# Retention q, k and gate columns as six transposed pairs of seven half-size products, values as row projections

## The chip, the cores and the metric

The kernel runs on one core of a Trainium2 chip. TensorE (PE in the profile) multiplies, VectorE (DVE) and ScalarE (ACT) work on its results, GpSimd (POOL) helps with elementwise work and issues some DMAs, SyncE (SP) issues most of them. The metric is the device time of one execution in microseconds (us).

## The reference, cut to what matters

One decoder layer over 1024 rows of width 1024. A combined projection of the modulated input feeds eight forgetting-attention heads ("fox", 64 wide) and four retention heads (128 wide). Retention is computed in chunks of 128 rows:

```
h  = modulate(x)                                  # 1024 x 1024
q, k, v, f, rq, rk, rv, rg = split(h @ w_in)      # widths 3 x 512, 8, 4 x 512
rq, rk = rotate(rq), rotate(rk)                   # cos and sin of the position
per retention head and chunk:
    out   = (rq rk^T * inner) rv + (rq * xi) state
    state = g_chunk * state + (rk * zeta)^T rv
ret = group_norm(out) * swish(rg)
fox = softmax(q k^T / 8 + decay(f), causal) v
x   = layer_norm(alpha*x + gate * (concat(fox, ret) @ w_out)), then the MLP in the same manner
```

Everything is float32. A product of two float32 matrices is made of three matmuls of rounded parts, hi*hi + hi*lo + lo*hi.

## The kernel before, in words

The modulated input stands in SBUF transposed, as eight tiles `hhi` (the rounded part) and eight `hlo` (the rest) of 128 features x 1024 rows. A row projection takes 128 columns of these as the stationary operand and a 512 wide weight tile as the moving one: 8 feature blocks x 3 matmuls = 24 matmuls give 128 rows x 512 columns in one PSUM bank (`three`).

**First phase.** For each feature block j, `h_load` brings two 512 KB tiles `ada1`, which make the modulation, the weights `wrr` (256 KB) and the input `xt` (512 KB); ACT and DVE make `hhi` and `hlo`, and PE multiplies seven of the eight row chunks with `w0`, 21 matmuls for each j, into seven PSUM banks. In the kernel before `w0` holds the q, k, v and gate columns of retention head 0. All loads of this phase stand in one order on SP. Behind the last `xt` come the weights of head 1 (`wrr_0` to `wrr_3`, 512 KB each), of which the first is cast on ACT ahead of `hhi` of j = 7.

**Retention rows.** For each head and chunk one row projection of 512 columns (q, k, v, gate of that head): a copy to SBUF, the rotation on DVE (and POOL), then `ret_a` (q and k turned by PE, k scaled on ACT as `kz`), `ret_b` (scores and state product), `ret_c` (output and statistics), `ret_swish`. Once eight chunks of a head are done, `ret_norm` makes scale and offset from the statistics (17 small DVE operations for a head), `ret_gate` applies them on ACT, two chunks in a step, and multiplies by the gate on POOL, and `ret_out` turns the result and stores it to `mixR`. A table of ticks sets which of these steps is written between which halves of the row projections.

**Values of fox.** Behind that 16 row projections of 256 or 264 columns (`v_proj`) make the fox values (kept in SBUF as `V2`) and the forget gate. Meanwhile 32 pieces of the modulation for later stages (`mod_piece`, one DVE operation of 128x1024 each) are worked off.

**Fox.** Then come the projections of fox head 0 (`fox_proj`, 24 matmuls of 512 columns for each half t of the rows, in four parts): t = 0 and one part of t = 1 ahead of the loop, the other three parts in the loop's steps i = 0 to 2, then score blocks, softmax, turns and products.

**What sets the order.** Operations issued through `in_turn`, `turn` and `vec` keep the order in which they are written, on PE and on DVE. In the first phase the loads on SP and the work of ACT are pinned in the same way (`queued`). What ACT, POOL and SP issue besides in this block is put in order by a scheduler at build time (the block is opened with `schedule_with_timeline_sim`); each engine then works through its own queue strictly in order.

## Time and profile before

| | before |
|---|---|
| three runs | 1214.98, 1216.07 and 1216.07 us; median 1216.07 us |
| profiled execution, first to last instruction (no other time of it is listed) | 1214.8 us |
| PE busy | 1198.3 us, 99% |
| DVE busy | 910.9 us, 75% |
| ACT busy | 653.9 us, 54% |
| POOL busy | 229.0 us, 19% |
| first phase | 0 to about 50.7 us |
| retention rows | 50.7 to 222.4 us |
| fox values | 222.4 to 272.3 us |
| fox head 0, its projections | from 272.3 us |

An engine's share is an average over all stages. A wait in a row stands behind the instruction that waited, with the engine that ended the wait. A matmul's row shows its time in the pipe, several overlap; how fast PE works is read from a run of them (12 in 2.75 us).

### The profile page before, as it was taken

Reading aid. Unit: us, or ns where it says so; the run is one execution under the profiler, and the core shown is the slowest. Engines: PE = TensorE matmul, PEld = TensorE weight load, DVE = VectorE, ACT = ScalarE, POOL = GpSimd, SP = SyncE. Lnnn points to the kernel's source line nnn. Section 1 sums busy time; section 2 is a strip of 40 time slices with the busy share of each in tenths; the row PEclk is TensorE's granted clock in tenths of the full one; section 3 lists DMA queues with packets and bytes.
Section 4 is the critical chain, followed back from the end, with each engine's and each line's share of the span. In section 5 each row is a group of like instructions: output and inputs, shape, how many; then the busy total and the mean of one; then the engine's idle time right before and its main releaser. Section 6 shows DMA issues by size and latency. Waiting matters only on the chain.

```text
span 1214.8 us, 17196 instructions
## 1 busy us (share of the span) xinstructions
PE 1198.3 (99%) x6005; PEld 1002.4 (83%) x6005; DVE 910.9 (75%) x1757; ACT 653.9 (54%) x1201; POOL 229.0 (19%) x274
## 2 busy tenths in 40 slices
...
GB/s 358 227 87 122 139 148 143 202 32 175 164 222 164 203 171 335 96 77 115 87 178 204 193 223 185 171 184 175 152 139 128 148 249 297 321 243 178 248 181 69
DMA packets 94279, 216.57 MB, mean 178 GB/s; under 512 B 10784, under 2 KB 17136, under 8 KB 94192
## 3 DMA queue, kind: packets, MB, share of 16 engines
...
## 4 chain that ended last, share of the span: by engine, by line
PE 87%; DMA 5%; DVE 4%; ACT 1%; issue 1%; SPq 0%; POOL 0%; DVEq 0%; ACTq 0%; POOLq 0%
PE rp L152 11%; PE dX L1489 7%; PE uX L1264 7%; PE uX L1263 7%; PE uX L1265 7%; PE dZ L1489 5%; PE uY L1263 5%; PE uY L1265 5%; PE uY L1264 5%; PE vp L152 4%; PE pv L851 3%; DMA ada<-in_ada_dram 3%; PE pt L835 2%; PE op L189 2%; PE op L191 2%; PE op L190 2%
## 5 line engine op out<-in xcount | busy, mean ns | idle before, releaser
L152 PE MATMUL rp<-wr,hhi 128*128 128x512 f32 x400 | 127.9, 401 | 0.0
L1475 DVE TENSOR_TENSOR dl<-dr,dh 128x1024 fp32r<-128x1024 f32 x66 | 80.3, 1237 | 36.3 <-ACT dh L1463 35.1
L813 POOL TENSOR_TENSOR S<-S,dn 128x128 f32<-128x128 f32 (+3 forms) x64 | 73.5, 1154 | 151.7 <-DVE dn L812 130.1
L1463 ACT CAST dh<-dr 128x1024 fp32r<-128x1024 f32 x58 | 59.6, 1051 | 65.7 <-DMA dr<-td 35.5
...
L152 PEld LDWEIGHTS rp<-wr,hhi 128*128 128x128 f32 x400 | 71.6, 189 | 12.7
L152 PE MATMUL rp<-wr,hlo 128*128 128x512 f32 x200 | 78.6, 393 | 0.0
L1489 PE MATMUL dX<-dh 128*128 128x512 f32 x176 | 68.5, 389 | 0.8 <-DVE ds L1641 0.8
L1489 PE MATMUL dX<-dl,dh 128*128 128x512 f32 x176 | 68.5, 389 | 0.0
L1489 PE MATMUL dX<-dh,dl 128*128 128x512 f32 x176 | 68.5, 389 | 0.0
L1278 ACT COPY u<-uX 128x512 f32<-128x512 f32 x44 | 25.8, 586 | 70.3 <-PE uX L1265 70.3
L152 DVE CUSTOM_DVE_ANT_0 ada<-ada,csb,bcol 128x1024 f32<-128x1024 f32 x46 | 60.1, 1309 | 3.0 <-DMA ada<-in_ada_dram 3.0
L842 DVE TENSOR_TENSOR pt<-pt,pt 128x512 fp32r<-128x512 f32 (+2 forms) x96 | 50.7, 549 | 10.2 <-ACT pt L841 9.1
L809 ACT ACTIVATE S<-S,mn 128x128 f32<-128x128 f32 (+3 forms) x64 | 49.9, 779 | 11.1 <-DVE mn L802 10.5
L765 PE MATMUL qk<-hhi,wqh 128*128 128x512 f32 x128 | 54.8, 428 | 0.4 <-DVE pt L828 0.4
L767 PE MATMUL qk<-hhi,wql 128*128 128x512 f32 x128 | 51.9, 405 | 0.0
L1489 PE MATMUL dZ<-dh 128*128 128x512 f32 x132 | 51.6, 391 | 0.0
L1489 PE MATMUL dZ<-dl,dh 128*128 128x512 f32 x132 | 51.4, 389 | 0.0
L1489 PE MATMUL dZ<-dh,dl 128*128 128x512 f32 x132 | 51.4, 389 | 0.0
L841 ACT CAST pt<-pt 128x512 fp32r<-128x512 f32 (+2 forms) x96 | 44.1, 478 | 13.4 <-PE pt L835 12.1
L189 PE MATMUL op<-wo,mxs 128*128 128x512 f32 x128 | 51.1, 399 | 0.0
L802 DVE CUSTOM_DVE_ANT_0 S<-ps,nb 128x128 f32<-128x128 f32 (+3 forms) x64 | 47.4, 741 | 4.2 <-PE ps L800 3.5
...
## 6 DMA issues: line engine op xcount, KB each, us to landing
...
```

Of the source, the lines that this page charges most:

```text
L152: order[key] = fn(*args, **kw)
L189: mm(pt, ahi, whi, start=start, stop=False)
L765: nc.tensor.matmul(pt, whi[:, j, :], hhi[j][:, sl], start=(j == 0), stop=False)
L767: nc.tensor.matmul(pt, wlo[:, j, :], hhi[j][:, sl], start=False, stop=(j == ND - 1))
L813: nc.gpsimd.tensor_tensor(out=Ssb[:, :span], in0=Ssb[:, :span], in1=den.to_broadcast([P, span]), op=ALU.mult,)
L842: nc.vector.tensor_tensor(out=dl, in0=src, in1=f(dh), op=ALU.subtract)
L1263: nc.tensor.matmul(pt, whi, bh, start=start, stop=False, skip_group_check=True)
L1264: nc.tensor.matmul(pt, whi, bl, start=False, stop=False, skip_group_check=True)
L1265: nc.tensor.matmul(pt, wlo, bh, start=False, stop=stop, skip_group_check=True)
L1463: nc.scalar.copy(hi, raw)
L1475: nc.vector.tensor_tensor(out=lo, in0=raw, in1=f(hi), op=ALU.subtract)
L1489: nc.tensor.matmul(pt, w_[:, 0, q], m_[:, 1, :], start=start and n_ == 0, stop=stop and n_ == 2, skip_group_check=True)
```

## The change

It does the following.

- `w0` of the first phase now holds the 512 value columns of fox; the chunks are taken in the order 4, 5, 6, 7, 0, 1, 2, and chunk 3 follows. `fv_out` splits them and stores them to DRAM (`V2d`); eight DMAs of POOL bring them back as `V2` at the end of the block.
- `w1` holds the retention values of all four heads: eight row projections of 24 matmuls, stored to `rv_d` and read back for each head by `r_begin`.
- The forget gate becomes two products of 16 matmuls (`forget_proj`, 16 or 8 rows x 512) and eight small turns.
- The 12 blocks of 128 columns of q, k and gate form six pairs. Each pair is computed transposed (features on the partitions, 1024 rows along the free axis) as seven products of half size, after Strassen and Winograd: the sums of weight halves are made on POOL (`rw_s`, `rw_d`, `rw_z`), the sums of the input's halves once by POOL and DVE (`t_sums`, `t_first`), and each product is 4 feature blocks x 3 = 12 matmuls. `r_evac` adds the products together.
- `t_first` overwrites the second halves of `hhi` and `hlo` of j = 0 to 3; `h12_save` stores them to DRAM before (8 x 256 KB, issued on SP), `h12_load` brings them back at the end with eight DMAs of POOL.
- The rotation works on transposed tiles: `spin` swaps the halves with two ACT copies and multiplies on POOL, `spin_end` does the rest on DVE. Of q and k only k is turned, and not in the last chunk. The gate (`swish`, `swish_end`, `r_gate`) is multiplied on DVE from PSUM.
- `r_norm` issues the eight ACT operations of a head (scale and offset, 128x128) in one step.
- Both halves t of the projections of fox head 0 stand at the end of the block, and the loop has none of head 0 left for i = 0 to 2.

The core of the diff (the removed functions are in the listing above):

```diff
+RPAIRS = [
+    [("q", 0), ("k", 0)], [("q", 1), ("k", 1)], [("g", 0), ("g", 1)],
+    [("q", 2), ("k", 2)], [("q", 3), ("k", 3)], [("g", 2), ("g", 3)],
+]
...
+    def h12_save(j):
+        for u, t in enumerate((hhi[j], hlo[j])):
+            nc.sync.dma_start(h12d[u, j], f(t[:, 512:S]))
...
+    def r_prod(p, g, half, pt, start, stop):
+        whi, wlo = W["r", p, g]
+        for j in (2 * half, 2 * half + 1):
+            bh, bl = r_moving(g, 0, j), r_moving(g, 1, j)
+            a, b = start and j == 0, stop and j == 3
+            in_turn(pt, whi[:, j, :], bh, start=a, stop=False, skip_group_check=True)
+            in_turn(pt, whi[:, j, :], bl, start=False, stop=False, skip_group_check=True)
+            in_turn(pt, wlo[:, j, :], bh, start=False, stop=b, skip_group_check=True)
...
+    def r_norm(h, part):
...
+        for c in range(NT):
+            o = st["o"][:, c, :]
+            nc.scalar.activation(o, o, AF.Identity, scale=r[:, c:c + 1], bias=mr[:, c:c + 1])
...
+    for b, c in enumerate(CO):
+        fv_out(c, first[b])
+    for j in range(4):
+        h12_save(j)
...
+    START = {0: 18, 1: 34, 2: 60, 3: 75}
+    for h in range(RH):
+        p = (0, 1, 3, 4)[h]
+        wide = (2, 2, 2, 1)[h]
+        at(START[h] - 2, r_begin, h)
+        for c in range(NT):
+            t = START[h] + wide * c
+            at(t, r_scores, h, c)
+            at(t + wide, r_state, h, c)
+            at(t + (5 if wide == 2 else 2), r_rows, h, c)
+        t = START[h] + 7 * wide + (6 if wide == 2 else 3)
+        at(t, r_norm, h, 0)
+        at(t + 1, r_norm, h, 1)
+        for n in range(2):
+            at(max(t + 3 + n, 14 * (2 if h < 2 else 5) + 17 + h % 2), r_gate, h, n)
+
+    GROUPS = (1, 2, 6, 5, 7, 3, 4)
...
+    for p in range(NP):
+        st = {"X": bank(f"rX{p}"), "YZ": bank2(f"rY{p}")}
+        for gi, g in enumerate(GROUPS):
...
+            for half in range(2):
+                tick = 14 * p + 2 * gi + half
+                emit(tick)
+                r_prod(p, g, half, pt, g in (1, 2, 5), g in (2, 3, 4))
+            r_evac(p, g, st, tick)
...
+            if gi % 2 == 1 or gi == 6:
+                mod_piece("VM")
...
+    tick = 14 * NP
+    for t in range(2):
+        for part in range(4):
+            emit(tick)
+            tick += 1
+            if (t, part) == (0, 2):
+                mod_rows(1)
+            fox_proj(0, w, T[0], t, part, in_turn)
```

SP's queue at the end of the first phase, before: `wrr_7` is the weight of j = 7 (named `wrr_7` with a number of the tile), `wrr_0_345` the first load of `w1`.

```order
L152 DMA xt_294<-in_xT_dram 128x1024
L152 DMA ada_7_0_327<-in_ada_dram 128x1024
L152 DMA ada_7_1_328<-in_ada_dram 128x1024
L152 DMA wrr_7_331<-in_w_ret_dram 128x512
L152 DMA xt_333<-in_xT_dram 128x1024
L152 DMA wrr_0_345<-in_w_ret_dram 128x1024
```

The same place in the changed kernel; `hlo_264`, `hhi_261` and `hlo_303` are tiles of j = 2 and 3.

```order
L158 DMA xt_294<-in_xT_dram 128x1024
L158 DMA ada_7_0_327<-in_ada_dram 128x1024
L158 DMA ada_7_1_328<-in_ada_dram 128x1024
L441 DMA h12d<-hlo_264 128x512
L441 DMA h12d<-hhi_261 128x512
L158 DMA wrr_7_331<-in_w_fv_dram 128x512
L158 DMA xt_333<-in_xT_dram 128x1024
L441 DMA h12d<-hlo_303 128x512
L158 DMA wrr_0_345<-in_w_rv_dram 128x1024
```

Three of the eight stores are seen here; the other five stand between the loads of j = 4 to 6, so all eight are ahead of `wrr_0_345`.

ACT where head 0 is normalised, before: `rst` rows of head 0 are scaled by `L504`, those of head 1 are at chunks 4 to 6.

```order
L432 ACTIVATE kz_5_1226<-rst_2_591,rc 128x128
L428 COPY qkT_4_1146<-pq_4_1143 128x256
L504 ACTIVATE rst_0_496<-rst_0_496,mr_1100,gr_1050 128x128 x2
L504 ACTIVATE rst_1_497<-rst_1_497,mr_1100,gr_1050 128x128 x2
L473 ACTIVATE rst_2_591<-rst_2_591 128x128
L178 CAST wr_6_1110<-wrr_6_1108 128x512
L178 CAST wr_7_1113<-wrr_6_1108 128x512
L466 COPY rst_0_589<-po_1_1129 128x128
L395 COPY rst_3_592<-rp_7_1116 128x512
L466 COPY rst_1_590<-po_2_1170 128x128
L432 ACTIVATE kz_6_1280<-rst_3_592,rc 128x128
```

ACT at that place in the changed kernel: `ro_1194` is the output of head 0, `kz_3_1670` the scaled k of chunk 3 of head 1, `rwD3h` the rounded weight sum of pair 3, `th` a tanh of the gate, `ru` the finished columns of a pair, `rX` a PSUM bank of a product.

```order
L634 ACTIVATE kz_2_1605<-pa_2_1600,rc 128x128
L660 COPY ro_1489<-po_0_1623 128x128
L554 CAST rwZ_1696<-rwa_1397 128x512
L686 ACTIVATE ro_1194<-ro_1194,mr_1639,gr_1608 128x128 x8
L520 CAST rwD3h<-rwb_1480 128x1024
L604 ACTIVATE th_1656<-ru_0_1475 128x512
L895 COPY ru_1_1476<-rX_1402 128x512
L634 ACTIVATE kz_3_1670<-pa_3_1665,rc 128x128
L660 COPY ro_1489<-po_1_1678 128x128
```

The eight operations of a head stand in one row of the queue, ahead of a cast, a tanh, a copy and `kz_3`; before they were in groups of two and four between the others.

DVE where head 2 is normalised, before: `gt`, `gr` and `wg` are the root's small tiles, `mr` the offset, the chunk operations are those of head 3.

```order
L152 TENSOR_SCALAR wg_1999<-wg_1999 128x8
L152 TENSOR_TENSOR gr_1996<-gr_1996,wg_1999 128x8
L152 TENSOR_SCALAR gr_1996<-gr_1996,rc 128x8
L152 SCALAR_TENSOR_TENSOR mr_2056<-mv_1200,gr_1996 128x8
L152 SCALAR_TENSOR_TENSOR rst_0_1824<-rst_0_1824 128x128
L152 TENSOR_TENSOR rst_1_1825<-rst_1_1825,trig 128x256
L152 TENSOR_TENSOR rst_1_1825<-rst_1_1825,rt_3_2071 128x2x64 x2
L152 ISA ada_2_3_2008,gcol<-ada_2_3_2008,csb,bcol 128x1024
L152 ISA gcol 128x1
L152 BN_STATS bs_1_2119<-po_1_2116 128x6
L152 BN_AGGR mv_1828<-bs_1_2119 128x2
```

DVE at that place in the changed kernel: `ru_0_2316` is a gate block of pair 5, `ISA ada` a `mod_piece`, `po_5` an output and `R_6` a state of head 3.

```order
L158 TENSOR_SCALAR wg_2508<-wg_2508 128x8
L158 TENSOR_TENSOR gr_2505<-gr_2505,wg_2508 128x8
L158 TENSOR_SCALAR gr_2505<-gr_2505,rc 128x8
L158 SCALAR_TENSOR_TENSOR mr_2548<-mv_2020,gr_2505 128x8
L158 TENSOR_TENSOR ru_0_2316<-rY_2238,r_5_2366 128x512
L158 ISA ada_3_6_2418,gcol<-ada_3_6_2418,csb,bcol 128x1024
L158 ISA gcol 128x1
L158 BN_STATS bs_5_2578<-po_5_2575 128x6
L158 BN_AGGR mv_2302<-bs_5_2578 128x2
L158 SCALAR_TENSOR_TENSOR R_6_2584<-R_5_2529,rc,pb_6_2582 128x128
L158 TENSOR_TENSOR sT_7_2588<-pa_7_2586,dec_2299 128x128
```

The statistics, the state and the masked scores of head 3's chunks now stand behind the small operations, an addition of 512 columns and a `mod_piece`; before a chunk of head 3 had its own projection between them.

More of the change, by code (lines that the diff above doesn't have):

```diff
@@ L420, with fv_out @@
-    turned = {}
-    def ret_a(h, c, st):
-        row = st["st"][c // 2][:, c % 2, :]
-        pq = bank(f"pq{h}_{c}")
-        turn(pq[:, 0:128], row[:, 0:P], ident)
-        turn(pq[:, 128:256], row[:, P:2 * P], ident)
-        qkT = tmp([P, 256], F32, f"qkT{h}_{c}")
-        turned["last"] = nc.scalar.copy(qkT, pq[:, 0:256])
-        st["qkT", c] = qkT
+    def fv_out(c, pt):
+        vs = slot("S" if c % 2 else "R", [P, FH // 2, 2, P], F32R, f"vs{c}")
+        hv = pt.rearrange("p (g o d) -> p g o d", o=2, d=64)
+        for o in range(2):
+            a, b = (0, 64) if o == 0 else (64, 0)
+            hi = vs[:, :, o, a:a + 64]
+            nc.scalar.copy(hi, hv[:, :, o, :])
+            vec(nc.vector.tensor_tensor, out=vs[:, :, o, b:b + 64],
+                in0=hv[:, :, o, :], in1=f(hi), op=ALU.subtract)
+        nc.sync.dma_start(V2d.rearrange("h p c d -> p h c d")[:, :, c, :],
+                          f(vs.rearrange("p g o d -> p (g o) d")))
@@ new lines, in mod_rows, with mod_piece, w_gate @@
+    def mod_rows(m):
+        pt = bank(f"gT{m}")
+        turn(pt[:ND, :P], gcol[:, m, :], ident)
+        row = tmp([ND, P], F32, f"grow{m}")
+        nc.scalar.copy(row, pt[:ND, :P])
+        nc.sync.dma_start(gates[m:m + 1, :].rearrange("o (j p) -> (o j) p", p=P), row)
+    def mod_piece(tag="R"):
+        n = mst.get("n", 0)
+        m, j = divmod(n, ND)
+        if m < 4:
+            mod_part(m, j, mst["next"])
+            mod_load(n + 1, tag)
+            mst["n"] = n + 1
+    def w_gate():
+        w = sp.tile([P, ND, 2, FH], F32R, tag="dec", bufs=1, name="wg")
+        raw = wgr[:, 0:64].rearrange("p (j h) -> p j h", h=FH)
+        nc.scalar.copy(w[:, :, 0, :], raw)
+        vec(nc.vector.tensor_tensor, out=w[:, :, 1, :], in0=raw,
+            in1=f(w[:, :, 0, :]), op=ALU.subtract)
+        return w.rearrange("p j u h -> p j (u h)")
@@ new lines, with forget_proj @@
+    L = cp.tile([P, NT, FH], F32, tag="L", name="L")
+    cum_d = dp.tile([64, P], F32, tag="cum_d", name="cum_d")
+    def forget_proj(n, wg):
+        sl = slice(n * 512, n * 512 + 512)
+        pt = bank(f"pf{n}")
+        for j in range(ND):
+            in_turn(pt[:2 * FH], wg[:, j, :], hhi[j][:, sl], start=(j == 0), stop=False,
+                    skip_group_check=True)
+            in_turn(pt[:FH], wg[:, j, 0:FH], hlo[j][:, sl], start=False, stop=(j == ND - 1),
+                    skip_group_check=True)
+        t = tmp([2 * FH, 512], F32, f"fT{n}")
+        nc.scalar.copy(t, pt[:2 * FH])
+        return t
@@ new lines, in forget_rows, with forget_out @@
+    def forget_rows(n, t, pt):
+        for i in range(4):
+            c = 4 * n + i
+            turn(pt[:, c * 2 * FH:(c + 1) * 2 * FH], t[:, i * P:(i + 1) * P],
+                 ident[:2 * FH, :2 * FH])
+    def forget_out(pt):
+        src = pt[:, 0:2 * FH * NT].rearrange("p (c u h) -> p c u h", u=2, h=FH)
+        vec(nc.vector.tensor_tensor, out=L, in0=src[:, :, 0, :],
+            in1=bfb.unsqueeze(1).to_broadcast([P, NT, FH]), op=ALU.add)
+        vec(nc.vector.tensor_tensor, out=L, in0=src[:, :, 1, :], in1=L, op=ALU.add)
@@ L636, in fox_w @@
-    def fox_w(h):
-        raw = slot("R", [P, ND, P], F32, f"wqkr{h}")
-        nc.sync.dma_start(raw, w_qk[h])
-        whi = slot("X", [P, ND, P], F32R, f"wqh{h}")
-        wlo = slot("X", [P, ND, P], F32R, f"wql{h}")
-        nc.scalar.copy(whi, raw)
-        for q in range(2):
-            sl = slice(4 * q, 4 * q + 4)
-            nc.vector.tensor_tensor(
-                out=wlo[:, sl, :], in0=raw[:, sl, :], in1=f(whi[:, sl, :]), op=ALU.subtract
-            )
-        return whi, wlo
-    L = cp.tile([P, NT, FH], F32, tag="L", name="L")
@@ new lines, in r_gate @@
+    def r_gate(h, n):
+        st, sl = sts[h], slice(n * 512, n * 512 + 512)
+        pt = bank(f"py{h}_{n}")
+        for i in range(4):
+            turn(pt[:, i * P:(i + 1) * P], st["o"][:, 4 * n + i, :], ident)
+        g = st["g"][:, sl]
+        vec(nc.vector.tensor_tensor, out=g, in0=pt, in1=g, op=ALU.mult)
+        nc.sync.dma_start(mixR[h, :, sl], g)
+    RANK = (r_begin, r_rows, r_state, r_scores, spin_end, swish_end, r_norm, r_gate)
+    for b, c in enumerate(CO):
+        fv_out(c, first[b])
```

599 lines of the change are left out of this document (328 added, 271 removed).

## The prediction

> **What bounds the kernel now.** First the page: the span, the busy shares and their course.
>
> ```profile
> span 1214.8 us, 17196 instructions
> PE 1198.3 (99%) x6005; PEld 1002.4 (83%) x6005; DVE 910.9 (75%) x1757; ACT 653.9 (54%) x1201; POOL 229.0 (19%) x274
> ```
>
> PE is busy nearly throughout, so work taken from it shortens the kernel as long as nobody else is late instead. Whether PE really never waits in the stage that is changed, and how near the others are, is read from windows (span, then busy time and count of PE, weight loads, DVE, ACT, POOL, then granted clock, DMA share, GB/s).
>
> ```profile
> 40.00:45.00 5.00, 5.00 (x23) 3.86 (x21) 4.25 (x8) 2.41 (x5) 0.00 (x0) 1.00 1.03 403
> 45.00:50.00 5.00, 4.45 (x20) 3.64 (x20) 3.35 (x6) 4.77 (x8) 0.00 (x0) 1.00 0.53 190
> ...
> 50.00:100.00 50.00, 50.00 (x264) 42.62 (x263) 30.12 (x103) 20.00 (x57) 11.41 (x18) 1.00 0.25 76
> 100.00:150.00 50.00, 50.00 (x273) 42.89 (x272) 37.80 (x122) 23.21 (x67) 21.44 (x31) 1.00 0.41 127
> 150.00:200.00 50.00, 50.00 (x262) 42.22 (x261) 31.38 (x95) 20.85 (x57) 21.47 (x32) 1.00 0.46 144
> 200.00:250.00 50.00, 50.00 (x351) 46.60 (x350) 35.89 (x123) 22.05 (x75) 11.33 (x18) 1.00 0.54 172
> ```
>
> From 50 to 250 us PE has not one idle spot; DVE stands at 60 to 76%, ACT under half. Up to 45 us the bound is another: the DMA engines are full (share 1.03 at 403 GB/s). The chain of waits, in order of time, shows where the two bounds meet and what a matmul costs.
>
> ```profile
> 34.30 8.95 DMA wrr<-in_w_ret_dram
> ...
> 43.80 0.61 ACT wr L152
> 44.41 1.15 ACT hhi L152
> ...
> 45.61 1.20 PE fa L152 x4
> ...
> 56.35 2.75 PE rp L152 x12
> ...
> 239.27 14.48 PE vp L152 x120
> ```
>
> The last round of the first phase begins at 45.61, behind `hhi`, behind a cast, behind a load. A matmul of 512 columns takes 2.75/12 = 0.229 us, one of 256 or 264 columns 14.48/120 = 0.121 us.
>
> **PE's work.** Behind the first phase the kernel before has 25 row projections of 24 (600 matmuls of 512 columns), 16 x 24 = 384 narrow ones, and 48 of fox head 0. The changed one has the row projection of chunk 3 (24), eight of retention values (192), the forget gate (32), six pairs of seven products of 12 (504), and the same 48. The difference: 752 x 0.229 - 600 x 0.229 - 384 x 0.121 = -11.7 us. The turns:
>
> ```profile
> 68.75 0.38 PE L152 MATMUL pS<-qkT 128*128 128x128 f32 x2
> 68.97 0.39 PE L152 MATMUL pS<-rst,kz 128*128 128x128 f32 x2
> 69.19 0.38 PE L152 MATMUL pq<-ident,rst 128*128 128x128 f32 x2
> 69.33 0.71 PE L152 MATMUL rp<-wr,hhi 128*128 128x512 f32 x2
> ```
>
> By the starts, a product of 128 columns (two records) takes 0.22 us and two turns 0.14. 64 become 28, so -36 x 0.07 = -2.5 us, and eight small turns of the gate add about 0.5: **-13.7 us** in all, if nobody is late. This holds to a few tenths, as PE waits for nothing there now.
>
> **The first phase.** Eight stores of 256 KB (2.1 MB) now stand on SP ahead of `wrr_0`, the load that releases the cast ahead of the last `hhi`. DMA is full there, so they cost 2.1 MB / 0.404 MB per us = 5.2 us on the path that PE waits for. If they fit beside the loads they cost nothing, and if stores are slower than loads a little more: 0 to 6, I take **+5.2**, since the row shows no spare share. Moving `trig` and `dec` out helps nothing: they were issued behind `wrr_0`.
>
> **The stage of products.** From here the question is what stands between PE's own instructions. Durations:
>
> ```profile
> L152 DVE CUSTOM_DVE_ANT_0 ada<-ada,csb,bcol 128x1024 f32<-128x1024 f32 x32 | 42.2, 1320 | 0.7 <-DMA ada<-in_ada_dram 0.7
> L152 DVE BATCH_NORM_STATS2 bs<-po 128x6 f32<-128x128 f32 x32 | 9.4, 294 | 17.3 <-PE po L152 17.0
> L152 DVE TENSOR_TENSOR sT<-pS,dec 128x128 f32<-128x128 f32 x32 | 8.6, 269 | 3.4 <-PE pS L152 3.4
> L152 DVE SCALAR_TENSOR_TENSOR R<-R,rc,pS 128x128 f32<-128x128 f32 x24 | 8.1, 338 | 0.0
> L152 DVE BATCH_NORM_AGGREGATE mv<-bs 128x2 f32<-128x6 f32 x32 | 5.8, 182 | 1.0
> L152 DVE TENSOR_SCALAR wg<-wg 128x8 f32<-128x8 f32 x12 | 3.5, 295 | 0.3
> L152 DVE TENSOR_TENSOR wg<-gr 128x8 f32<-128x8 f32 x12 | 3.3, 276 | 0.2
> L152 DVE TENSOR_TENSOR wg<-wg,gt 128x8 f32<-128x8 f32 x12 | 3.0, 251 | 0.3
> L644 DVE TENSOR_TENSOR wql<-wqkr,wqh 128x512 fp32r<-128x512 f32 x4 | 2.6, 683 | 0.5 <-ACT wqh L641 0.5
> L152 DVE TENSOR_TENSOR gr<-gr,wg 128x8 f32<-128x8 f32 x12 | 2.6, 218 | 0.3
> ...
> L152 DVE TENSOR_SCALAR gr<-gr,rc 128x8 f32<-128x8 f32 x4 | 1.1, 270 | 0.1
> L152 DVE TENSOR_SCALAR gt<-gt,rc 128x8 f32<-128x8 f32 x4 | 0.9, 229 | 0.1
> L152 DVE TENSOR_SCALAR gt<-mv,rc 128x8 f32<-128x8 f32 x4 | 0.9, 225 | 0.0
> L152 DVE TENSOR_SCALAR gr<-gt 128x8 int32<-128x8 int32 x4 | 0.7, 172 | 0.1
> L152 DVE SCALAR_TENSOR_TENSOR mr<-mv,gr 128x8 f32<-128x8 f32 x4 | 0.7, 164 | 0.1
> ```
>
> The 17 small operations of one head's normalisation take 3 x (0.276 + 0.251 + 0.295 + 0.218) + 0.225 + 0.229 + 0.172 + 0.270 + 0.164 = 4.18 us. An operation of 512 columns takes 0.68, a `mod_piece` 1.32. On ACT and POOL:
>
> ```profile
> L395 ACT COPY rst<-rp 128x512 f32<-128x512 f32 x25 | 14.6, 585 | 26.3 <-PE rp L152 26.3
> L504 ACT ACTIVATE rst<-rst,mr,gr 128x128 f32<-128x128 f32 x32 | 13.3, 487 | 2.0 <-DVE mr L152 2.0
> L432 ACT ACTIVATE kz<-rst,rc 128x128 f32<-128x128 f32 x28 | 11.3, 405 | 31.1 <-DVE rst L152 17.5 <-PE pS L152 13.5
> ...
> L641 ACT CAST wqh<-wqkr 128x1024 fp32r<-128x1024 f32 x2 | 2.1, 1050 | 1.6 <-DMA wqkr<-in_w_qk_dram 1.6
> ...
> L179 POOL TENSOR_TENSOR wr<-wrr,wr 128x512 fp32r<-128x512 f32 x16 | 20.4, 1299 | 20.3 <-ACT wr L178 20.3
> ```
>
> Eight operations of `r_norm` are 8 x 0.487 = 3.9 us of ACT in one piece. At five places I add up what has to run between two instructions of PE, and what PE has to do meanwhile:
>
> - **Head 0 normalised, in pair 2.** From the end of the seventh product (g = 7): DVE does an addition 0.68, R 0.34, sT 0.27, the 17 small ones 4.18, bs and aggr 0.48, a swish 0.68, to `mr`: 6.6 us. Then ACT: eight operations 3.9, cast of `rwD3` 1.05, tanh 0.59, copy 0.59, `kz_3` 0.41: 6.5 us. PE waits for `kz_3` with `pb_3`; until then it has 24 matmuls (5.5 us) and some small ones (1.6 us), 7.1 us. Late by 13.1 - 7.1 = **6.0**.
> - **Head 1, start of pair 4.** From the end of the product g = 3: DVE 0.68 + 1.32 + 2 x 0.68 + 4.18 = 7.5, then four operations on ACT 1.9 until `py_0` is through. PE has 18 matmuls, 4.1 us. **5.4**.
> - **Head 2, among the chunks of head 3.** These follow each other at half the distance. From the end of g = 7 of pair 5 to `R_6` DVE has two whole chunks (bs, aggr, R, sT: 1.08 each) and most of a third (0.81), two additions and a swish (2.0), the small ones 4.18 and a `mod_piece` 1.32: 10.5. PE has 18 matmuls and 13 small ones, 6.9 us. **3.6**.
> - **Head 3, behind the last product.** From `po_6`: bs, aggr twice, two swishes, a `mod_piece`, the small ones, and 0.7 us for a tanh that stands behind the eight operations of head 2, 8.5 us; ACT 1.9. PE has 30 matmuls and the turns, 7.9 us. **2.5**.
> - **The first scores (pair 1).** `pa_0` waits for the last quarter of k: ACT 1.05 + 0.59 and two half swaps, POOL 2.6 (a tile of 1024 columns, taken as twice 1.3), 1.3 for the next sum and 1.3 for the product, DVE 0.68: 6.9 against 24 matmuls, 5.5. **1.4**.
>
> Together 18.9 us. Elsewhere DVE is the next bound. In a pair with six chunks it has four `mod_piece` (5.3), work of 14 times 512 columns (9.5), the chunks (6.5) and a normalisation (4.2), 25.5 us; PE has 84 matmuls and six chunks of 0.95, 24.9. It can be late by 1 or 2 us more between pairs 1 and 2, or the waits above may let it catch up. I take nothing for it. The bounds of these waits are 8 (if half of what is named is already done) and 25 (if the cross-engine hops and DVE's backlog come on top).
>
> **The start of fox.** Now 18 matmuls stand among the first score steps (4.1 us):
>
> ```profile
> 280.82 0.47 PE L796 MATMUL ps<-ks,qh 128*128 128x256 f32 x2
> ...
> 286.79 0.28 PE L835 MATMUL pt<-ident,S 128*128 128x128 f32 x1
> ```
>
> From scores to the first turn pass 6.0 us, filled with them. After the change only six of the next head are there. Between 0 and 4.1, I take half: **+2.0**. The reloads by POOL I cost at nothing: PE has eight parts (48 matmuls, 11 us) to cover them. If that is not enough, head 0's products wait for `V2`, some 2 us.
>
> **The sum.** -13.7 + 5.2 + 18.9 + 2.0 = +12.4, against the profiled span of 1214.8: 1227.2. The runs lie 0.2 to 1.3 us above that span, so **1228 us**.
>
> **Rivals.**
> - *The waits at the normalisations do not reach PE.* ACT is under half busy, and the same 17 and 8 operations of a head cost PE nothing in the rows above. If all four places (17.5 us) vanish, the time is 1228 - 17.5 = 1210.5; it is faster once they make less than 3 us. Against it: in the kernel before 24 matmuls stood between two chunks, now 12 or 6, and ACT's eight operations are in one piece. Chance 0.22.
> - *Half of it.* Waits of about 8 us and stores that cost half: 1228 - 11 - 2.5 = 1214.5 to 1218, within 0.2% of before. 0.10.
> - *PE's clock falls behind a long wait.* The granted clock is 1.00 in every row above, and before there is no long wait to see it fall. The two waits over 5 us would each be followed by some 3.4 us at half pace, if that is what happens: +3.4, 1231.5; with DVE's backlog 1235. 0.12.
>
> The Trainium skill, page "TensorE: Matmul & The Clock Gate", section "Part 1: The HAM clock gate (the "warmup" mystery)", states that an idle window of about 3.4 us puts the array on half its clock until it has been busy for as long; by it that last rival would be the forecast. No wait of before is long enough to show it.
>
> My forecast (1220 to 1232) has 0.56. A difference of 0.2% (2.4 us) is about what a measurement of this kernel can tell from no change. Faster: 0.22; within: 0.10; slower: 0.68. The range that leaves two in ten out reaches into the first rival and over the last: 1208 to 1236.
>
> **What would show it.** PE's idle time in front of `pb_3` of head 1, `py_0` of head 1, `po_6` of head 3 and `py_0` of head 3, released by ACT (or by DVE for `po_6`); the first phase ending some 5 us later than 50.7, with the stores between the loads; idle PE behind the first `ps`. The PE work is right if busy time falls by about 14 us. If PE is idle for less than 10 us in the stage of products, the hand sums of waits are wrong; if `fa` of the last round begins near 45.6, the stores cost nothing.

## The result and the profile after

The changed kernel takes 1267.17 us (median of four runs, 1266.41 to 1272.82), the kernel before 1216.07: a ratio of 1.0429, 95% interval 1.0407 to 1.0450. Slower was forecast, but by 12 us and not by 51; the range ended at 1236.

The page of the changed kernel, span, busy shares, and the slices of PE and of its granted clock:

```profile
span 1264.4 us, 16514 instructions
PE 1203.7 (95%) x5745; PEld 987.3 (78%) x5745; DVE 967.9 (77%) x1662; ACT 671.2 (53%) x1132; POOL 273.9 (22%) x246
...
PE   8999798698999999999999999999999999999997
...
PEclk9999799898999999999999999999999999999999
```

PE has less to multiply, yet its busy time rose from 1198.3 to 1203.7 us: a matmul at a lower clock is busy for longer (0.63 us in its row instead of 0.39). DVE's rose by 57 us. The two deepest holes in PE's slices (7 and 6 tenths, ahead of the last slice) lie between 120 and 260 us, and the windows show their size (columns as in the prediction):

```profile
50.00:100.00 50.00, 47.26 (x203) 35.15 (x204) 36.04 (x55) 26.51 (x53) 12.89 (x7) 0.97 0.60 188
100.00:150.00 50.00, 44.61 (x188) 36.05 (x187) 37.09 (x66) 14.85 (x22) 19.28 (x12) 0.93 0.53 182
150.00:200.00 50.00, 41.58 (x213) 34.57 (x214) 38.93 (x78) 19.18 (x40) 26.12 (x15) 0.93 0.37 122
200.00:250.00 50.00, 35.93 (x174) 29.56 (x173) 40.45 (x84) 23.44 (x49) 22.98 (x14) 0.86 0.35 113
```

Before, PE was busy for 50 of 50 us in each of these, at a clock of 1.00. Now it is idle up to 14 us of 50, and no other engine is busy for more than 41. That is the picture of chains between engines, not of one full engine. PE's timeline names the waits (start, duration, instruction, and in brackets the idle time ahead of it with the engine that ended it):

```profile
50.80 1.20 PE L158 MATMUL fa<-wr,hhi 128*128 128x512 f32 x4 [1.22 <-ACT hhi L158]
...
129.24 0.80 PE L158 MATMUL rY<-hhi,rwS0h 128*128 128x512 f32 x1 [4.03 <-DVE ru L158]
...
154.99 0.76 PE L158 MATMUL pa<-ru,ru 128*128 128x128 f32 x2 [6.35 <-DVE ru L158]
...
208.16 0.49 PE L158 MATMUL pb<-rv,kz 128*128 128x128 f32 x2 [3.81 <-ACT kz L634]
...
246.61 1.62 PE L158 MATMUL py<-ident,ro 128*128 128x128 f32 x4 [10.25 <-ACT ro L686]
...
289.67 0.49 PE L158 MATMUL pb<-rv,kz 128*128 128x128 f32 x2 [3.01 <-ACT kz L634]
...
310.79 0.49 PE L158 MATMUL po<-rv,sT 128*128 128x128 f32 x2 [1.98 <-DVE R L158]
...
331.89 0.66 PE L969 MATMUL ps<-ks,qh 128*128 128x384 f32 x1 [3.15 <-DVE mn L975]
```

**An account of the 49.6 us between the two profiled spans.** PE's work -13.7 (the prediction's figure; the last experiment below bears it out within 1.4 us); the last round of the first phase begins at 50.80 and not at 45.61, +5.2; idle time of PE between 50 and 330 us, summed over windows of 10 us, 39.9 against 0.6, +39.3; between 330 and 1100 us 4.2 against 2.0, +2.2. The clock: each such window's busy time times what its granted clock lacks of 1.00, summed, 14.0 against 0. Together 47.0; 2.6 us stay unassigned.

So three things are to be explained: why the waits hold twice what the hand sum gave, what the clock does, and whether the first phase's 5 us count.

### Where the longest wait comes from

The head's small operations run just ahead of the wait of 10.25 us. DVE's timeline of the changed kernel (start, duration):

```profile
234.89 1.60 DVE L158 TENSOR_TENSOR ru<-ru,sw 128x512 f32<-128x512 f32 x1
236.42 2.31 DVE L158 TENSOR_SCALAR gt<-mv,rc 128x8 f32<-128x8 f32 x1
238.76 1.18 DVE L158 TENSOR_SCALAR gt<-gt,rc 128x8 f32<-128x8 f32 x1
239.98 1.19 DVE L158 TENSOR_SCALAR gr<-gt 128x8 int32<-128x8 int32 x1
241.20 0.17 DVE L158 TENSOR_TENSOR wg<-gr 128x8 f32<-128x8 f32 x1
241.40 1.12 DVE L158 TENSOR_TENSOR wg<-wg,gt 128x8 f32<-128x8 f32 x1
242.55 1.19 DVE L158 TENSOR_SCALAR wg<-wg 128x8 f32<-128x8 f32 x1
243.77 0.17 DVE L158 TENSOR_TENSOR gr<-gr,wg 128x8 f32<-128x8 f32 x1
```

and POOL's timeline at the same time:

```profile
235.94 2.76 POOL L524 TENSOR_TENSOR rwD4l<-rwb,rwD4h 128x1024 fp32r<-128x1024 f32 x1
238.66 1.25 POOL L591 TENSOR_TENSOR sw<-sw,tab 128x512 f32<-128x512 f32 x1
239.88 1.25 POOL L535 TENSOR_TENSOR rws<-rwb 128x512 f32<-128x512 f32 x1
241.21 1.28 POOL L537 TENSOR_TENSOR rws<-rws,rwa 128x512 f32<-128x512 f32 x1
242.45 1.26 POOL L544 TENSOR_TENSOR rwb<-rwa,rwb 128x512 f32<-128x512 f32 x1
```

Five operations on eight columns (the two `gt`, `gr` and two `wg`), which take 0.17 to 0.23 us when POOL is idle, end when POOL's operation ends: 236.42 + 2.31 = 238.73 beside 235.94 + 2.76 = 238.70; 239.94 beside 239.91; 241.17 beside 241.13; and so on. Four of the five read a single tile. The `wg` at 241.20 began 0.01 us ahead of POOL's next operation and was not held. The row at 243.77, with POOL done, is back at 0.17. The 17 operations take 9.6 us and not the 4.2 of the prediction. That is one place; how much of the whole loss is this, the experiments tell.

### The profile page after: what moved, and what is told of

Same layout as the page of the kernel before. It is cut to its first block, busy times and chain, and to the rows that moved or that the text cites. A ratio compares the mean times of both kernels' runs of the same rounds, so it can differ in the third digit from the quotient of the medians.

```text
span 1264.4 us, 16514 instructions
## 1 busy us (share of the span) xinstructions
PE 1203.7 (95%) x5745; PEld 987.3 (78%) x5745; DVE 967.9 (77%) x1662; ACT 671.2 (53%) x1132; POOL 273.9 (22%) x246
## 4 chain that ended last, share of the span: by engine, by line
PE 63%; DVE 15%; DMA 13%; ACT 5%; issue 3%; SPq 1%; DVEq 0%; POOL 0%; ACTq 0%; POOLq 0%
PE uX L1434 6%; PE uX L1435 6%; PE uX L1433 6%; PE uY L1434 4%; PE uY L1435 4%; PE uY L1433 4%; PE rX L158 3%; DMA dr<-td 3%; PE rY L158 3%; PE pv L1024 3%; DMA dr<-in_w_down_dram 3%; DMA ada<-in_ada_dram 2%; DVE dl L1645 2%; PE dX L1659 2%; PE pt L1008 2%
## 5 line engine op out<-in xcount | busy, mean ns | idle before, releaser
L1645 DVE TENSOR_TENSOR dl<-dr,dh 128x1024 fp32r<-128x1024 f32 x66 | 80.1, 1237 | 38.3 <-ACT dh L1633 37.2
L158 DVE CUSTOM_DVE_ANT_0 ada<-ada,csb,bcol 128x1024 f32<-128x1024 f32 x46 | 67.1, 1468 | 9.9 <-DMA ada<-in_ada_dram 9.9
L1015 DVE TENSOR_TENSOR pt<-pt,pt 128x512 fp32r<-128x512 f32 (+2 forms) x96 | 50.7, 550 | 10.1 <-ACT pt L1014 9.1
L182 PE MATMUL op<-wo,mxs 128*128 128x512 f32 x128 | 51.0, 399 | 0.0
L184 PE MATMUL op<-wo,mxs 128*128 128x512 f32 x128 | 50.0, 390 | 0.0
L183 PE MATMUL op<-wo,mxs 128*128 128x512 f32 x128 | 49.9, 390 | 0.0
L1500 ACT ACTIVATE y<-ua,cw 128x1024 f32<-128x1024 f32 x22 | 27.4, 1245 | 41.6 <-DVE ua L1495 41.6
L1024 PE MATMUL pv<-pt,V 128*128 128x256 f32 x320 | 49.1, 292 | 0.3 <-DVE pt L1015 0.2
L830 PE MATMUL qk<-hhi,wqh 128*128 128x512 f32 x112 | 48.7, 434 | 0.3 <-DVE mixF L1031 0.3
L1725 POOL TENSOR_TENSOR fo<-fo,frow 128x512 f32<-128x512 f32 x7 | 10.3, 1484 | 172.1 <-ACT fo L1724 172.1
```

What stands on the lines that cost most here:

```text
L158: order[key] = fn(*args, **kw)
L182: mm(pt, ahi, whi, start=start, stop=False)
L184: mm(pt, alo, whi, start=False, stop=stop)
L1015: nc.vector.tensor_tensor(out=dl, in0=src, in1=f(dh), op=ALU.subtract)
L1024: nc.tensor.matmul(pv[:, :256], V2[h][:, kb, :], pts[kb // 4][u][:, kb % 4, :], start=(kb == 0 and u == 0), stop=(kb == nkb - 1 and u == 1),)
L1645: nc.vector.tensor_tensor(out=lo, in0=raw, in1=f(hi), op=ALU.subtract)
```

## The experiments

Each changes the changed kernel, except where another is named. Times are medians of four runs, ratios are against the kernel before on the same chip.

### POOL writes, but reads nothing

The five kinds of elementwise operation that POOL has in the stage of products become memsets of the same tiles. The weights' sums and low halves and the sine products are left out; PE, ACT and DVE do the same instructions.

```diff
-  nc.gpsimd.tensor_tensor(out=lo, in0=raw, in1=f(hi), op=ALU.subtract)
+  nc.gpsimd.memset(f(lo), 0.0)
...
-  nc.gpsimd.tensor_tensor(out=sw, in0=sw, in1=tab[n][:, 1, :], op=ALU.mult)
+  nc.gpsimd.memset(sw, 0.0)
```

> In the stage of products every elementwise operation of POOL (the sine products of the rotation, the sums of weight halves and their low parts) is left out, and a memset of the same tile stands in its place: POOL then only writes SBUF there and reads none of it. The changed kernel takes 1267 us. If DVE and POOL hold each other up (in the changed kernel an addition of 512 columns took 1.60 us beside POOL and 0.69 alone), DVE's operations fall back to 0.69, 20 to 26 us of DVE time go, and with it 15 to 30 us of the whole: 1237 to 1252. If the waits come from the normalisation's own chain (17 small operations, eight activations in one piece) and DVE is slow for another reason, the time stays within 5 us: 1262 to 1267. POOL's operations also become shorter (1.3 us to perhaps 0.6), which is worth 1 to 3 us in the chain of the rotation in either case.

Measured: 1240.87 us (1238.65 to 1244.82), ratio 1.0210 (1.0190 to 1.0230): 26 us of the 51 are gone. DVE's groups between 110 and 330 us (busy time, mean in ns, then idle time ahead), of the changed kernel:

```profile
L158 DVE TENSOR_TENSOR ru<-ru,sw 128x512 f32<-128x512 f32 x16 | 18.2, 1139 | 1.5
...
L158 DVE TENSOR_TENSOR rwZ<-rwa,rwZ 128x512 fp32r<-128x512 f32 x6 | 10.1, 1678 | 0.0
...
L158 DVE TENSOR_TENSOR ru<-rX,r 128x512 f32<-128x512 f32 x6 | 4.2, 692 | 6.1 <-PE rX L158 6.1
```

and of this run:

```profile
L158 DVE TENSOR_TENSOR ru<-ru,sw 128x512 f32<-128x512 f32 x16 | 11.1, 691 | 1.5
...
L158 DVE TENSOR_TENSOR ru<-rX,r 128x512 f32<-128x512 f32 x6 | 4.1, 691 | 6.6 <-PE rX L158 6.6
L158 DVE TENSOR_TENSOR rwZ<-rwa,rwZ 128x512 fp32r<-128x512 f32 x6 | 4.1, 676 | 0.0
```

The same operations on the same shapes: those that read two tiles of SBUF go from 1.14 and 1.68 us back to 0.69 and 0.68, those that read a PSUM bank (`rX`) and one tile take 0.69 us in both. DVE's busy time in the whole falls from 967.9 to 932.0 us. And PE's timeline of this run:

```profile
188.84 0.49 PE L158 MATMUL pb<-rv,kz 128*128 128x128 f32 x2 [3.79 <-ACT kz L630]
...
221.78 1.64 PE L158 MATMUL py<-ident,ro 128*128 128x128 f32 x4 [4.74 <-ACT ro L682]
...
263.33 0.49 PE L158 MATMUL pb<-rv,kz 128*128 128x128 f32 x2 [2.94 <-ACT kz L630]
...
284.45 0.49 PE L158 MATMUL po<-rv,sT 128*128 128x128 f32 x2 [1.96 <-DVE R L158]
```

The wait of 10.25 is 4.74, those of `pa` (6.35) and `rY` (4.03) are gone, the others stay. (At `rY` DVE is late behind a load, 3.74 us; with memsets it waits 3.71 us for the same load, but 6.4 us earlier, at 114.69 instead of 121.10, and PE, 2.7 us earlier, does not notice.) Idle time of PE from 50 to 330 us falls from 39.9 to 21.1 us, the clock's share of the loss from 14.0 to 8.3.

### The same with each memset twice

A memset is also shorter than the sum that it replaces (0.53 us for 512 columns and 0.96 for 1024, against 1.25 and 2.36 at the least). Is it POOL's shorter chain that helps?

```diff
-  nc.gpsimd.memset(f(lo), 0.0)
+  for _ in range(2):
+      nc.gpsimd.memset(f(lo), 0.0)
```

> As the run with memsets (1240.9 us), which leaves POOL's elementwise work of the products out, but each memset stands twice, so that POOL is busy for 1.05 us in place of 0.53 per 512 columns (1.3 for the real operation) and the chain through it is about as long as in the changed kernel. If POOL's reading of SBUF beside DVE's was the cost, nothing comes back: 1239 to 1244. If the shorter chain through POOL was it, half or more of the 26 us comes back: 1253 to 1262.

Measured: 1244.53 us (1237.67 to 1246.24), ratio 1.0223 (1.0193 to 1.0252). 22.6 of the 26.3 us stay gained, just above the first band, and the interval overlaps the last one's. By its rows POOL's 52 operations of the stage take 93 us in the changed kernel, 33 as single memsets and 65 as double ones, so about half of the length is back; scaled to the whole of it, the 3.7 us would be 7 (an estimate), and the intervals allow nothing at all. A memset also needs none of the tiles that a sum needs. But nobody waited for these sums: in the list of waits of the changed kernel between 55 and 335 us no wait of PE or DVE ends with POOL, and one of ACT (3.7 us; 2.6 with single memsets). So what POOL reads beside DVE is most of the 26 us, and the length of its chain is a few us.

### POOL's sums on DVE

```diff
-  nc.gpsimd.tensor_tensor(out=s[:, 0:4, :], in0=b[:, 0:4, :], in1=b[:, 4:8, :], op=ALU.add)
+  vec(nc.vector.tensor_tensor, out=s[:, 0:4, :], in0=b[:, 0:4, :], in1=b[:, 4:8, :], op=ALU.add)
...
-  nc.gpsimd.tensor_tensor(out=sw, in0=sw, in1=tab[n][:, 1, :], op=ALU.mult)
+  vec(nc.vector.tensor_tensor, out=sw, in0=sw, in1=tab[n][:, 1, :], op=ALU.mult)
```

> The changed kernel with all of POOL's elementwise work of the products (sums of weights, their low halves, sine products) on DVE: nothing is left out. By DVE's rows with POOL idle (0.68 us for 512 columns, 1.31 for 1024) that is 6 x 5.3 + 16 x 0.68 = 43 us more work for DVE. If DVE's load were the cause of the long waits, they grow: 1275 to 1295. If DVE and POOL holding each other up is the cause, DVE gets about 35 us back and the chains lose POOL's 2.4 us steps: 1250 to 1265, with the low halves' and the small operations' mean back at 0.68 and 0.3 us.

Measured: 1284.70 us (1282.91 to 1286.48), ratio 1.0564 (1.0546 to 1.0581): the time is in the other theory's band. The rows are as the first said, though. The page of this run:

```profile
PE 1208.4 (94%) x5745; PEld 991.1 (77%) x5745; DVE 969.0 (76%) x1714; ACT 671.8 (52%) x1132; POOL 181.5 (14%) x194
```

By their rows the moved operations take DVE 42 us, and its busy time is 969.0 against 967.9. So some 41 us of DVE's busy time in the changed kernel was time in which POOL held it up; the run with memsets, in which POOL still writes, gave 36. What my expectation left out is DVE's order. Its waits (what waited, for whom, total us, times, longest):

```profile
DVE sw L158 <- ACT sw L590: 19.7, 14, 1.9
```

and two rows of its timeline:

```profile
121.43 0.69 DVE L158 TENSOR_TENSOR sw<-sw,tab 128x512 f32<-128x512 f32 x1 [1.32 <-ACT sw L590]
...
132.07 1.23 DVE L158 TENSOR_TENSOR rwS1l<-rws,rwS1h 128x1024 fp32r<-128x1024 f32 x1 [1.11 <-ACT rwS1h L520]
```


The half swaps (`sw`) and the casts (`rwS1h`) are made by ACT; POOL waited for them beside DVE, and now DVE waits itself, 19.7 us for `sw` and 1.1 to 1.4 us ahead of eleven of the twelve low halves, with all that is queued behind. PE waits longer for it: 51.5 us of idle time between 110 and 330 us against 37.2. This reading of the 17 us is from the rows; no run moved the subtractions away from their casts.

### The normalisation spread over four ticks

The prediction blamed the eight activations of a head in one piece. Here they are issued two in a tick, behind the last `kz`.

```diff
-        for c in range(NT):
-            o = st["o"][:, c, :]
+    def r_scale(h, c):
+        st = sts[h]
+        r, mr, o = st["r"], st["mr"], st["o"][:, c, :]
+        with tc.issue_after(turned["last"].ins):
...
+        for c in range(NT):
+            at(t + 1 + c // 2, r_scale, h, c)
```

> The eight activations of a head's normalisation are issued two by two over four ticks and pinned behind the last scaled k, so that for head 0 six of them no longer stand ahead of kz_3 of head 1; nothing is left out. If the piece of eight is what PE waits for, its wait at pb_3 (3.8 us) falls under 1.5 us and the slow clock behind it goes: -4 to -6 us, 1261 to 1263. If the waits come from DVE and POOL holding each other up, only that one place gains, at most 3 us, and the others (py_0 of head 1, 10.3 us; the first scores, 6.4 us) stay as they are: 1264 to 1267.

Measured: 1266.90 us (1265.58 to 1271.11), ratio 1.0427 (1.0407 to 1.0446). The wait at `pb_3` of head 1 falls from 3.81 to 2.18 us, `py_0` keeps 10.24, and the time stays. By the two profiled runs the gain lives until `py_0` (245.01 against 246.61 us) and is lost ahead of `pb_0` of head 3 (290.92 against 289.67), though the waits between are the same (2.15 and 3.15 against 2.14 and 3.01). What differs there is the clock: windows of 5 us between 245 and 290 lose 4.2 us to it, against 1.7 in the changed kernel.

### The first phase

First the eight stores are put behind the loads on SP:

```diff
-            nc.sync.dma_start(h12d[u, j], f(t[:, 512:S]))
+            queued("SP", nc.sync.dma_start, h12d[u, j], f(t[:, 512:S]))
```

> The eight stores of the second halves of hhi and hlo (2.1 MB) are issued behind the last load of the first phase; nothing is left out. If they cost the first phase what was forecast, its last round begins at 45.6 to 46.5 us in place of 50.8, and the whole is 4 to 5 us faster: 1262 to 1263. The rival: the transfers that follow (the fox values' stores and the weights, DMA share 1.0 from 60 to 80 us) are then later by as much, and a wait of PE on them takes back 2 to 5 us: 1264 to 1267.

Measured: 1265.91 us (1260.65 to 1269.12), ratio 1.0408 (1.0380 to 1.0436). The first row projection starts at 53.3 us (55.7 in the changed kernel, 50.5 in the one before): the stores are 2.4 us of the 5.2, and the rest has another cause. Then, in addition, POOL's sums of the inputs are held back until the last `hlo` is there:

```diff
+        if j == 0:
+            gate = small([P, 1], "gate")
+            queued("POOL", nc.gpsimd.tensor_tensor, out=gate, in0=f(hlo[7][:, 0:1]),
+                   in1=f(hlo[7][:, 0:1]), op=ALU.subtract)
-        nc.gpsimd.tensor_tensor(out=e1, in0=e1, in1=o1, op=ALU.subtract)
+        queued("POOL", nc.gpsimd.tensor_tensor, out=e1, in0=e1, in1=o1, op=ALU.subtract)
```

> As the run with the eight stores behind the loads (1265.9 us; its first phase still ended 2.6 us later than before the change), and POOL's eight subtractions of the input's halves begin only when the last tile hlo is done; nothing is left out. If they held DVE up in the first phase (its sums of 1024 columns took 1.71 us there, 1.31 later), the first row projection behind the phase starts at 50.7 to 51.3 in place of 53.3 and the whole is 2 to 3 us faster: 1262.5 to 1264. If something else made the phase longer, or the time returns later: 1265 to 1267.

Measured: 1264.25 us (1259.42 to 1265.62), ratio 1.0382 (1.0358 to 1.0407). The row projections start at 50.7, as before the change: the other half of the 5 us were POOL's sums beside DVE (in the changed kernel two of the modulation's operations, at 39.02 and 44.20 us, take 2.30 beside them, here 1.28). But a row of PE's timeline shows a new wait soon behind,

```profile
59.29 0.71 PE L158 MATMUL rp<-wr,hhi 128*128 128x512 f32 x2 [3.03 <-DVE vs L158]
```

the wait at `rY` is 4.87 instead of 4.03, and `pa` keeps 6.35. The sums hold DVE up later instead: its six `wr` from 48.14 us on take 8.08 us (4.81 in the changed kernel, 3.69 before). Of 5 us 3 are won by the medians, with an interval that touches the changed kernel's.

### One decay table

The single tile `dec` is loaded again for each head once the last scores of the head before have used it; head 3's first `pb` waits for that (3.01 us): DVE's `sT` for the load, ACT's `kz` for `sT`, `pb` for `kz`.

```diff
-        st["dec"] = sp.tile([P, P], F32, tag="dec", bufs=1, name=f"dec{h}")
-        nc.sync.dma_start(st["dec"], decay[h])
+        if h == 0:
+            dec0.append(sp.tile([P, P], F32, tag="dec", bufs=1, name="dec0"))
+            nc.sync.dma_start(dec0[0], decay[0])
+        st["dec"] = dec0[0]
```

> The changed kernel with head 0's decay table for all four heads, so that three loads into the one decay tile go (heads 1 to 3 are computed with head 0's decay). If the wait of head 3's first scores (3.01 us of PE ahead of pb, held by that load) is worth its size: 1264, and that wait under 0.7 us. If it is given back, since head 3's later steps wait for DVE anyway: 1266 to 1268.

Measured: 1264.18 us (1260.75 to 1268.88), ratio 1.0398 (1.0366 to 1.0430). The wait falls from 3.01 to 1.00, less than expected, and in the profiled run `rY` waits 6.17 us. The interval overlaps the changed kernel's: inconclusive by itself.

### Keeping the clock up

Behind most long waits the clock is low. PE's timeline of the changed kernel behind the wait of 4.03 us,

```profile
129.83 0.63 PE L158 MATMUL rY<-hlo,rwS0h 128*128 128x512 f32 x1
130.26 0.63 PE L158 MATMUL rY<-hhi,rwS0l 128*128 128x512 f32 x1
```

shows a matmul each 0.43 us instead of 0.227. Ten of them, until 133.67, cost 2.0 us. Windows behind four waits, of 1.22, 3.81, 2.14 and 1.98 us:

```profile
96.00:100.00 4.00, 4.00 (x13) 3.15 (x12) 3.77 (x5) 1.15 (x3) 4.00 (x2) 0.57 0.29 88
...
208.00:213.00 5.00, 4.84 (x19) 4.13 (x20) 4.88 (x9) 1.42 (x5) 3.69 (x3) 0.66 0.32 105
...
278.00:283.00 5.00, 4.68 (x27) 4.13 (x28) 4.21 (x11) 2.39 (x6) 0.00 (x0) 1.00 0.00 0
...
310.00:316.00 6.00, 5.21 (x20) 4.42 (x21) 4.36 (x15) 3.75 (x10) 2.29 (x5) 0.72 0.50 146
```

To keep PE busy, matmuls whose result nobody reads are issued into the bank ahead of the waiting product, 22 at `pa_0` of head 0, 12 at `pb_3` and 38 at `py_0` of head 1, 16.5 us of PE's time.

```diff
+    def keep_warm(pt, n):
+        for _ in range(n):
+            in_turn(pt, hhi[7][:, 0:P], hhi[7][:, 0:512], start=True, stop=True,
+                    skip_group_check=True)
```

> At the three longest waits of PE (first scores of head 0, pb_3 of head 1, py_0 of head 1) 22, 12 and 38 matmuls that nobody reads are put ahead of the waiting one, into the bank that it overwrites: 16.5 us more work for PE, in places where it waits 20.4 us. If the granted clock falls because PE is idle there (it is 0.50 to 0.79 in the 6 us behind each wait), the clock stays at 1.0 and the whole becomes 3 to 7 us faster although PE does more: 1260 to 1264. If the slow clock has another cause, or PE is not what is waited for behind those waits, the time stays or rises: 1266 to 1270.

Measured: 1264.28 us (1260.27 to 1268.57), ratio 1.0401 (1.0369 to 1.0432), granted clock 0.988 instead of 0.982. Unclear by itself. The clock itself answers: from 150 to 160 us it is 1.00 where it was 0.66, from 205 to 215 1.00 for 0.83, from 240 to 250 0.83 for 0.50. The same on the kernel with memsets, 14 at `pb_3` of head 1, 11 at `pb_0` and 7 at `po_6` of head 3, 18 at `py_0` of head 1:

> As the run with memsets (1240.9 us), and 14, 11, 18 and 7 matmuls that nobody reads ahead of the four instructions at which PE still waits there (pb_3 of head 1: 3.8 us, pb_0 of head 3: 2.9, py_0 of head 1: 4.7, po_6 of head 3: 2.0): 11.4 us more work for PE. DVE is not held up by POOL here, so PE's clock should show alone: if idle PE slows its clock and that is on the path, 4 to 8 us go, 1233 to 1237. If it is not on the path: 1240 to 1243.

Measured: 1237.90 us (1230.07 to 1238.85), ratio 1.0165 (1.0133 to 1.0197) against 1.0210 without. PE does 50 x 0.229 = 11.5 us more and the kernel takes 3 us less by the medians (the two intervals overlap between 1.0190 and 1.0197), a little above the 1233 to 1237 expected. The clock's loss between 50 and 330 us falls from 8.3 to 3.2 us, so idle PE does lower the clock; that no more than some 3 us show in the time is not explained by a run. The seven ahead of `po_6` filled nothing: they write its bank, and waited 1.96 us for it themselves.

### The single terms together

If the spread normalisation, the first phase and the decay table give nothing because the next wait takes it back, they should count where the waits are shorter. All three edits on the kernel with memsets:

> POOL's elementwise work of the products replaced by memsets (as before, weights' sums and sine products are left out) together with the three edits that gave little alone: the eight activations of a head spread over four ticks, the stores and the input sums of the first phase behind the loads, one decay table. If these costs are real but hidden behind the long DVE chains, they now count: from 1240.9 down by 2 (spread), 3 (decay), 3 to 5 (first phase) and what the clock gets back, 1228 to 1234. If they are given back here too: 1238 to 1241.

Measured: 1234.28 us (1231.41 to 1237.41), ratio 1.0150 (1.0124 to 1.0176), 6.6 us under the kernel with memsets alone, with intervals that do not overlap, and just above the 1228 to 1234 that was expected. On the changed kernel the three gave 0.3, 2.9 and 3.0 us by the medians, 6.2 together: each was too small to stand out, and this run does not show that they count more where the waits are shorter. In PE's timeline of this run

```profile
184.85 0.49 PE L158 MATMUL pb<-rv,kz 128*128 128x128 f32 x2 [2.18 <-ACT kz L638]
...
217.77 1.63 PE L158 MATMUL py<-ident,ro 128*128 128x128 f32 x4 [4.74 <-ACT ro L694]
...
277.55 0.49 PE L158 MATMUL po<-rv,sT 128*128 128x128 f32 x2 [1.98 <-DVE R L158]
...
299.15 0.69 PE L979 MATMUL ps<-ks,qh 128*128 128x384 f32 x1 [3.14 <-DVE mn L985]
```

there remain the waits that the prediction had, and none of over 1.0 us that it had not, but for 3.0 us in the first rows.

### Plain blocks in place of the seven products

The twelve column blocks as four plain products of half a block each, 576 matmuls instead of 504. No sums, no stores and reloads of the input's halves; POOL keeps only the 16 sine products. (In the first of the two kernels the second block of each pair has the sign that the seven products' tables expect.)

```diff
-    def r_prod(p, g, half, pt, start, stop):
-        whi, wlo = W["r", p, g]
-        for j in (2 * half, 2 * half + 1):
+    def r_direct(p, u, n, half, pt):
+        whi, wlo = W[p, u]
+        for j in range(4 * half, 4 * half + 4):
```

> The 12 column blocks transposed as in the change, but as plain products: 576 matmuls in place of 504, no sums of weight or input halves, no second halves stored and brought back, no additions of products; the low parts of the weights on DVE, POOL has the 16 sine products alone. Nothing of the result is left out. PE has 72 matmuls more, 16.5 us. If POOL's work beside DVE's is the main cost, it goes with it, and the first phase is 5 us shorter: 1233 to 1250. If the waits lie in the layout (rotation, normalisation, scores of transposed tiles), the time is that of the change plus 16.5 less the 5 of the first phase: 1274 to 1282.

Measured: 1227.55 us (1225.84 to 1230.63), ratio 1.0097 (1.0079 to 1.0114): 39.6 us faster than the changed kernel, with 72 x 0.229 = 16.5 us more for PE, and below both bands of the expectation. Transposed tiles, rotation and normalisation are the same here, so by themselves they do not cost it; sums, additions and stores go at once, and the run does not split the time among them. The waits are gone but for the start of fox, 3.14 us ahead of its second `ps`. Then three of the eight parts of head 0's projection go back among the first score steps:

```diff
-            if h > 0:
-                fox_proj(h, w, T[h], 1, i + 1)
+            fox_proj(h, w, T[h], 1, i + 1)
...
-    for t in range(2):
-        for part in range(4):
+    for t, part in ((0, 0), (0, 1), (0, 2), (0, 3), (1, 0)):
```

> The twelve plain blocks again, with the signs of the tables and of the normalisation put back to plain ones (the plain blocks before this had the negative ones of the seven products), and with three of the eight parts of fox head 0's projection back among the first score steps. If the start of fox is what the plain blocks still lose against the kernel before: PE's idle time between 270 and 310 us falls from 4.6 to under 1 us, and the time from 1227.5 to 1222 to 1224. If the loss is elsewhere: 1227 or more.

Measured: 1223.42 us (1222.69 to 1224.47), ratio 1.0061 (1.0046 to 1.0076). Windows of the first plain kernel

```profile
270.00:310.00 40.00, 36.84 (x187) 29.62 (x186) 26.44 (x82) 23.69 (x55) 10.57 (x15) 0.96 0.76 249
```

and of this one:

```profile
270.00:310.00 40.00, 39.33 (x215) 32.23 (x214) 29.73 (x92) 25.29 (x58) 11.80 (x15) 1.00 0.78 250
```

PE's idle time there falls from 3.2 us (the expectation had 4.6) to 0.7. The move of fox's projection costs 4.1 us by the two medians: 2.5 of idle time and 0.04 x 37 = 1.5 of clock. What is left against the kernel before is 8.0 us by the profiled spans: 2.8 of PE's work (16.5 - 13.7), 2.2 more idle time between 110 and 330 us (2.8 against 0.6), 0.4 of clock behind the first phase (in the last 13 us), and a first row projection 1.2 us later, at 51.7. That is 6.6, so the -13.7 of the prediction holds within some 1.4 us. No version here beats the kernel before.

## Why the prediction was wrong, point by point

The waits of the prediction, with what the changed kernel and the kernel with memsets show (us):

| place | predicted | changed | memsets |
|---|---|---|---|
| first scores, `pa_0` | 1.4 | 6.35 | under 0.5 |
| head 0 normalised, `pb_3` of head 1 | 6.0 | 3.81 | 3.79 |
| head 1, `py_0` at pair 4 | 5.4 | 10.25 | 4.74 |
| head 2, `po_6` of head 3 | 3.6 | 1.98 | 1.96 |
| head 3, `py_0` | 2.5 | under 0.5 | under 0.5 |
| start of fox | 2.0 | 3.15 | 3.14 |
| sum | 20.9 | 25.5 | 13.6 |
| idle time 50 to 330 us | | 39.9 | 21.1 |

- **The step that failed: "Durations".** The waits were summed from mean rows of the kernel before, as if an operation kept its length. In the changed kernel POOL has 36 sums and subtractions and 16 sine products of 1.25 to 3.4 us in the stage, and beside them DVE's operations of 512 columns take 1.1 to 1.7 us instead of 0.68, and small ones up to 2.31 instead of 0.2. POOL was not idle before either (104 operations, 70 us between 50 and 275 us, but of 0.67 us on average), and single rows of DVE and POOL showed the hold-up there already:

```profile
194.62 1.30 DVE L152 TENSOR_SCALAR wg<-wg 128x8 f32<-128x8 f32 x1
194.57 1.31 POOL L530 TENSOR_TENSOR wv<-wvr,wv 128x520 fp32r<-128x520 f32 x1 [1.02 <-DVE wg L152]
```

One of twelve such `wg` took 1.30 us, the median 0.17; the mean of 0.295, which the prediction used, hides it. With POOL's reads the kernel is 26 us longer than without. That idle time is then 21.1 us, beside my 20.9, is luck: at the six places named 13.6 appeared, and the rest at places that I had not named (the decay table's 2.94 us). The terms listed for the first scores also add up to 7.5 us without the two half swaps, and not to 6.9. The sentence "Elsewhere DVE is the next bound [...] I take nothing for it" belongs to the same step: `rY` waited 4.03 us there. The Trainium skill, page "SBUF — State Buffer", section "Who interferes with whom", states that DVE and GpSimd share a pair of SBUF ports under an exclusive lock: a DVE instruction with two SBUF inputs contends with a GpSimd instruction that reads SBUF, not with one that only writes, and the second to issue waits for the whole of the first. The rows of 512 columns agree: 1139 ns with sums on POOL, 691 with memsets, 692 with one input in PSUM; and the held ones end with POOL's operation. The page has one more case, DVE in a mode that uses both port pairs, which contends in any case. The small operations with one tile would need it: four of the five held ones above, and `gt<-mv,rc`, which took 1.48 us beside a memset. No run shows in which mode they were.
- **The clock.** The third rival came true beside the forecast and not in its place. The sum had nothing for it, and the rival 3.4 us for two waits; the windows give 14.0, as seven of the eight waits over 1.9 us between 50 and 335 us were followed by some 5 us of low clock, and the shorter waits were not expected to be. Of the 39 us by which the kernel missed the forecast, 26 go with POOL's reads (5.7 of the 14.0 among them); with memsets 13 are left, of which the windows give 8.3 to the clock. The Trainium skill, page "TensorE: Matmul & The Clock Gate", section "Part 1: The HAM clock gate (the "warmup" mystery)", has an idle window of about 3.4 us ahead of the half clock. The half pace agrees (0.43 against 0.227 us); the length doesn't fit as a length of one wait, since 1.98 us were followed by a clock of 0.72, and 2.14 us by 1.00; with the normalisation spread the same place waited 2.15 us, and the clock behind it was 0.81 to 0.85.
- **The first phase, +5.2.** The size was right (5.19) by luck, the cause by half: 2.4 us are the stores, the rest is again POOL beside DVE. The 5 us are not simply part of the sum: taken out alone they give 3 by the medians.
- **The activations in one piece** were the argument for the largest wait (6.0). The wait is 3.8, and spreading them gives no time in the changed kernel that its runs can tell.
- **The start of fox** was priced at 2.0, with 4.1 as the upper end: it is 4.1, 3.15 of wait and the rest of clock.
- **PE's work, -13.7,** holds within 1.4 us, by the plain blocks.
- **The rivals in which the waits do not reach PE** fell: of 18.9 us named in the stage of products, 22.4 appeared.

Open: 2.6 us of the account; why DVE's `mod_piece` stands 3.7 us behind a load (no run took these loads away); what decides whether a wait of 2 us lowers the clock; and how much of the 17 us of the kernel with sums on DVE are the waits in its queue.
